# The opening of a two-layer encoder and its first w_down loads: sink values later, first weight slab first, products of zeros, four loads due earlier

## The chip, the cores and the metric

One core of a Trainium2 chip runs the whole program. The metric is the device time of one execution in microseconds (us). Five engines work side by side, each with its own queue of instructions, which it takes in order: TensorE (PE, with its weight loads as PEld), VectorE (DVE), ScalarE (ACT), GpSimd (POOL) and SyncE (SP). DMAs are issued from the queues of SP, ACT and POOL.

## What is computed

The reference is an encoder trunk of two layers over 512 tokens of width 1024, all in float32. Cut to what matters here:

```python
for l in range(DEPTH):                                   # 2
    h = rms_norm(x, attn_norm_g[l])
    qa, ka, va, qb, kb, vb, ga, gb = split(h @ w_in[l])  # 1024 x 4352
    ya = window_gqa(rope(norm(qa)), rope(norm(ka)), va, sink_a[l]) @ w_proj_a[l]
    yb = neighbourhood_attn(norm(qb), norm(kb), vb, rel_bias_b[l]) @ w_proj_b[l]
    x = x + (sigmoid(ga) * ya + sigmoid(gb) * yb) @ w_out[l]
    h = rms_norm(x, ffn_norm_g[l])
    u = silu(h @ w_gate[l]) * (h @ w_up[l])              # 1024 x 2816
    x = x + u @ w_down[l]                                # 2816 x 1024
```

## The kernel before

Activations lie transposed: the 1024 features are eight chunks of 128 partitions, the 512 tokens are the columns. Each float32 operand of a product is split in two parts, a high one rounded to the narrower type (fp32r) and a low one that holds the rest, and each product is three products on PE: high by high, high by low and low by high. The high part is made by ACT (a cast), the low part by DVE (a subtraction); for most weights the DMA itself makes it (ACT writes the negated high part, an accumulating DMA from GpSimd's queue adds the weight).

**The order of work.** The function `trunk` is run twice. In the first run nothing is emitted: an engine model with costs decides in which order the chains of attention work are placed between the main products, and which buffers of two arenas in SBUF can share a place (`Layout.pack`). In the second run the instructions are emitted in that order. Weight loads stand in a plan: `slab` gives each a due time on a running count of TensorE's work (`total`), `LEAD_H` (23 us) before use for the load and `LEAD_L` (15 us) before use for the low part, shifted by `later_h` and `later_l`. All these loads go out from GpSimd's queue, in the order in which they fall due.

**The opening.** The first product block (`token_matmul` with `begin`) starts while the input is still arriving. For each of the eight chunks k, `start(nrm, k)` turns the chunk of x that was loaded (`xin[k]`) with four transposes on PE, has ACT write the high part (`xh`, scaled by the norm's gain), the float32 copy `xT` and its square, and DVE write the low part `xl` and add up the squares; `first_parts(k)` splits the chunk's weights (ACT the cast `h`, DVE `lo`). A chunk has four groups of three products, one for each block of 128 tokens; the first group of chunk k stands before the transposes of chunk k+1 and the other three behind them. `first_load(0)` loads the first slab of w_in in two halves from ACT's queue, `first_load(1)` to `(3)` the others from GpSimd's; `x_load` loads the eight chunks of x from SP's queue. The norm gains of both norms lie in one tile `vec`, which one transpose on PE turns to columns (`vecT`). Another tile, `vec2`, holds the small gains of the heads and the token positions; it is turned by `chain_tables`, which then makes the tables of sine and cosine on DVE (it needs the constants `cst`), and which also writes `nsnk`, the negated sink values, from `snk`.

**The start of the FFN.** The blocks of w_gate and w_up are multiplied by a scheme of seven block products (`m` from `ORDER`, 24 instructions each on PE); the results of some are copied on as starting values of others (`seed`, `fetch`, `seed_c`; `seed_c` is a DVE addition that reads the bank which the next block product writes). In the first such block the low parts come by DMA from GpSimd's queue (`low_by_transfer`). Between the block products stand those with w_down (`d` steps); their four first slabs (for f0 = 0) are planned in `plan_ffn`:

```python
if c % 2 == 0:
    slab(n, 256, [(0, a["w_down"][l][P * f0 : P * (f0 + n), P * c : P * c + 256])], 0, 3.0, 2.0)
```

Of the kernel before, what the change touches and what calls it, by code (L numbers as in the profile page):

```python
# [12 lines left out]
F32 = mybir.dt.float32  # L13
# [3 lines left out]
ALU = mybir.AluOpType  # L17
AX = mybir.AxisListType

P = 128  # L20
# [4 lines left out]
NB = S // P  # L25
# [184 lines left out]
def trunk(ctx: ExitStack, tc: tile.TileContext, a: dict, out: bass.AP, lay: Layout):  # L210
    nc = tc.nc
    PS = bass.MemoryType.PSUM
    cp = ctx.enter_context(tc.tile_pool(name="cp", bufs=1))
# [7 lines left out]
    def nm(s):  # L221
        uid[0] += 1
        return f"{s}_{uid[0]}"
# [24 lines left out]
    def mm_bank():  # L248
        return pm.tile([P, S], F32, tag="mm", name=nm("mm"))

    def at_bank():
        return pa.tile([P, S], F32, tag="at", name=nm("at"))
# [83 lines left out]
    T = Engine(nc.tensor, "pe")  # L336
    V = Engine(nc.vector, "dve")
    A = Engine(nc.scalar, "act")
    G = Engine(nc.gpsimd, "pool")
    Q = Engine(nc.sync, "dma")  # L340
    AQ = Engine(nc.scalar, "dma")
# [86 lines left out]
    def at_pos(t, f):  # L428
        bisect.insort(due, (t, len(seq), f))
        seq.append(0)  # L430
# [19 lines left out]
    def slab(n, width, src, units, later_h=0.0, later_l=0.0, on_engines=False):  # L450
        i = len(plan)
        plan.append((n, width, src))
        if on_engines:
            at_pos(total[0] - LEAD_R, lambda: w_raw(i))
            at_pos(total[0] - LEAD_P, lambda: w_parts(i))
        else:
            at_pos(total[0] - LEAD_H + later_h, lambda: w_load(i))
            at_pos(total[0] - LEAD_L + later_l, lambda: w_low(i))
        total[0] += units * UNIT
# [34 lines left out]
    def plan_ffn(l):  # L494
        plan_pair(a["w_gate"][l], 0, KD, on_engines=True)
        plan_pair(a["w_up"][l], 0, KD)
        for step in ffn_steps():
            if step[0] == "m":
                _, q, w, m = step
                if m == ORDER[0]:  # L500
                    t = total[0]
                    early = 18.0 if q == 0 and w == "w_gate" else 0.0
                    quads[l, q, w] = Quad(a[w][l], 256 + 512 * q, t - early, early > 0.0)
                quads[l, q, w].due(m, total[0] - early)
                early = max(0.0, early - 1.2)
                total[0] += 24 * 0.12
            else:
                _, f0, n, c = step
                if c % 2 == 0:
                    slab(n, 256, [(0, a["w_down"][l][P * f0 : P * (f0 + n), P * c : P * c + 256])], 0, 3.0, 2.0)  # L510
                total[0] += n * UNIT

    highs, lows, raws, used = {}, {}, {}, [0]
# [1 line left out]
    def w_raw(i):  # L515

        n1, n2, ((_, ap),) = plan[i]
        raws[i] = buf([n1, n2])
        Q.dma_start(raws[i], ap.rearrange("(k p) n -> p k n", p=P))

    def w_parts(i):
        n1, n2, _ = plan[i]
        highs[i], lows[i] = buf([n1, n2], F32R), buf([n1, n2], F32R)
        A.copy(highs[i], raws[i])
        soon(lambda: V.tensor_tensor(lows[i], raws[i], highs[i].bitcast(F32), ALU.subtract), 1.2)
# [3 lines left out]
    def first_load(i):  # L529

        n1, n2, ((_, ap),) = plan[i]
        raws[i] = buf([n1, n2])
        ap = ap.rearrange("(k p) n -> p k n", p=P)
        if i:
            GQ.dma_start(raws[i], ap)
        else:
            for k in range(2):
                AQ.dma_start(raws[i][:, k], ap[:, k])
        highs[i], lows[i] = buf([n1, n2], F32R), buf([n1, n2], F32R)

    def first_parts(k):
        raw, h, lo = raws[k // 2][:, k % 2], highs[k // 2][:, k % 2], lows[k // 2][:, k % 2]
        A.copy(h, raw)
        V.tensor_tensor(lo, raw, h.bitcast(F32), ALU.subtract)

    def w_load(i):

        if i not in highs:
            n1, n2, src = plan[i]
            highs[i] = buf([n1, n2], F32R)  # L550
            for at, ap in src:
                n = ap.shape[1]
                GQ.dma_start(highs[i][:, :, at : at + n], ap.rearrange("(k p) n -> p k n", p=P))
# [133 lines left out]
    ident = cst[:, C_ID : C_ID + P]  # L687
    rev = cst[:, C_REV : C_REV + P]
    rev2 = cst[:, C_REV + 64 : C_REV + 64 + P]
    maskA = cst[:, C_MA : C_MA + 3 * P]  # L690
    vec = cp.tile([32, P], F32, tag="vec", name="vec")
    vec2 = cp.tile([P, P], F32, tag="vec2", name="vec2")
    vecT = cp.tile([P, 32], F32, tag="vecT", name="vecT")
    vec2T = cp.tile([P, P], F32, tag="vec2T", name="vec2T")
    ones = cp.tile([P, 2], F32, tag="ones", name="ones")
    magic = cp.tile([P, 32], I32, tag="magic", name="magic")
    G.memset(vec2, 0.0)
    G.memset(ones, 1.0)
    G.memset(magic, 0x5F3759DF)
# [3 lines left out]
    def x_load(c):  # L703
        t = act().rearrange("p (b n) -> p b n", b=NB)
        Q.dma_start(t, xv[:, :, P * c : P * c + P])
        xin.append(t)


    Q.dma_start(ident, a["consts"][:, :P])
    for i, n in enumerate(("attn_norm_g", "ffn_norm_g")):  # L710
        AQ.dma_start(vec[16 * i : 16 * i + 16], a[n].rearrange("l (k p) -> (l k) p", p=P))
    first_load(0)
    for c in range(KD):
        x_load(c)
    posi = cp.tile([P, P], I32, tag="posi", name="posi")
    for h in range(2):
        GQ.dma_start(
# [12 lines left out]
    gqa = cp.tile([P, 2, DEPTH, HD], F32, tag="gqa", name="gqa")  # L730
    for i, n in enumerate(("q_norm_a", "k_norm_a")):
        GQ.dma_start(gqa[:, i], a[n].rearrange("l d -> (l d)").unsqueeze(0).to_broadcast([P, DEPTH * HD]))
    snk = cp.tile([P, DEPTH, 8], F32, tag="snk", name="snk")
    GQ.dma_start(snk, a["sink_a"].rearrange("l h -> (l h)").unsqueeze(0).to_broadcast([P, DEPTH * 8]))
    GQ.dma_start(cst[:, P:], a["consts"][:, P:])
    warm = cp.tile([P, 2], F32, tag="warm", name="warm")
    A.copy(warm, ones)
    ps = at_bank()
    T.transpose(ps[:, :32], vec, ident[:32, :32])
    V.tensor_copy(vecT, ps[:, :32])  # L740

    def gain(norm, k):
        c = 16 * (norm % 2) + 8 * (norm // 2) + k
        return vecT[:, c : c + 1]

    xT = [buf([S]) for _ in range(KD)]
    nsnk = cp.tile([P, DEPTH, 8], F32, tag="nsnk", name="nsnk")
    gb = cp.tile([P, DEPTH], F32, tag="gb", name="gb")
    trig = cp.tile([P, 2, NB, 32], F32, tag="trig", name="trig")

    def chain_tables():
        yield Need("dve", [posi, snk, gqa])
        V.tensor_copy(vec2[64:68], posi[64:68])
        V.tensor_scalar(nsnk, snk, -1.0, None, ALU.mult)
        yield Need("pe", [vec2], [at_slots])
        at_slots.take()
        ps = at_bank()
        T.transpose(ps[:, :P], vec2, ident)
        yield Need("dve", [ps])
        V.tensor_copy(vec2T, ps[:, :P])  # L760
        at_slots.give(clock["dve"])
        posf = vec2T[:, 64:68]
        V.scalar_tensor_tensor(gb, vec2T[:, 0:2], HD ** -0.5, vec2T[:, 2:4], ALU.mult, ALU.mult)
        v3 = lambda t: t[:, : NB * 32].rearrange("p (b f) -> p b f", b=NB)
        ang = v3(act())
        for b in range(NB):
            V.tensor_scalar(ang[:, b, :], cst[:, C_INV : C_INV + 32], posf[:, b : b + 1], None, ALU.mult)
        yield Need()
        for i, shift in enumerate((0.25, 0.0)):
            n, r = v3(act()), v3(act())  # L770
            V.tensor_scalar(n, ang, INV_2PI, shift, ALU.mult, ALU.add)
            V.tensor_scalar(n, n, ROUND_MAGIC, None, ALU.add)
            V.tensor_scalar(n, n, -ROUND_MAGIC, None, ALU.add)
            yield Need()
            V.scalar_tensor_tensor(r, n, -TWO_PI_1, ang, ALU.mult, ALU.add)
            V.scalar_tensor_tensor(r, n, -TWO_PI_2, r, ALU.mult, ALU.add)
            V.scalar_tensor_tensor(r, n, -TWO_PI_3, r, ALU.mult, ALU.add)
            yield Need()
            if shift:
                V.tensor_scalar(r, r, HALF_PI, None, ALU.add)  # L780
            V.tensor_scalar(r, r, PI_LO, -PI_LO, ALU.min, ALU.max)
            A.activation(trig[:, i], r, AF.Sin)
            yield Need()
        done.add("trig")


# [387 lines left out]
    def start(nrm, k):  # L1174

        ps = at_bank()
        for b in range(NB):
            T.transpose(ps[:, P * b : P * b + P], xin[k][:, b, :], ident)
        if k:
            first_parts(k)  # L1180
        A.activation(held(nrm.xh[k]), by_columns(ps), AF.Copy, scale=gain(0, k))
        if not k:
            first_parts(k)
        A.copy(held(xT[k]), by_columns(ps))
        V.scalar_tensor_tensor(nrm.xl[k], xT[k], gain(0, k), nrm.xh[k].bitcast(F32), ALU.mult, ALU.subtract)
        sq = act()
        A.activation(sq, xT[k], AF.Square)
        if nrm.acc is not None:
            V.tensor_tensor(sq, sq, nrm.acc, ALU.add)
        nrm.acc = sq  # L1190
        if k == KD - 1:
            done.add("acc0")
# [528 lines left out]
```

## Time and profile before

| | before |
|---|---|
| time, median of 3 runs | 1389.4 us (1389.08 to 1389.6) |
| time of the profiled execution | 1389.13 us |
| its span, first to last instruction | 1387.4 us |
| TensorE busy in the span | 1370.7 us (99%) |
| VectorE, ScalarE, GpSimd busy | 910.7, 708.3, 317.3 us |

The profiled execution is 1.7 us longer than its span, and 0.3 us below the median. In the rows further down a time at a row's start is in us from the span's start. A row of the timeline reads: start, length, engine, line, operation, out<-in, shapes, how many were merged (x4), and in brackets how long the engine had been idle before it and what ended that. An engine with a small q (SPq, ACTq) only issues a DMA. All of the kernel's instructions are recorded at one helper's line, L310, so tiles tell them apart: `arena` is a buffer in SBUF, `at` and `mm` are banks in PSUM; where two tiles have names that differ by a number only (`vec`, `vec2`) the profile gives both as `vec`.

### The profile page before, as it was taken

The numbers are of one execution on the slowest core, as the hardware profiler recorded it, in microseconds if no ns is written. First come the engines' busy times: TensorE is split into PE (matmuls) and PEld (weight loads), VectorE is DVE, ScalarE is ACT, GpSimd is POOL, SyncE is SP. The second block draws the span as 40 slices with busy tenths as digits, with TensorE's granted clock in tenths as the row PEclk, the third lists the DMA queues.
The fourth block names the chain that finished last, engine by engine and source line by source line (L and its number), as shares of the span: only waits on it lengthen the run. The fifth ranks groups of instructions, "written<-read, shape, count | busy, mean of one in ns | idle before, by whom it ended". The sixth has DMA issues, their size and how long they took to land.

```text
span 1387.4 us, 20895 instructions
## 1 busy us (share of the span) xinstructions
PE 1370.7 (99%) x8042; PEld 1211.2 (87%) x8042; DVE 910.7 (66%) x1702; ACT 708.3 (51%) x1171; POOL 317.3 (23%) x326
## 2 busy tenths in 40 slices
PE   8999999999999999999999999999999999999998
PEld 6888888888899999999888888888888999999996
DVE  5875878555976657575648667784578757575663
ACT  6476667634643333343545675675356434333441
POOL 4542222310221110111353422223012110111110
PEclk9999999999999999999999999999999999999999
DMA  8998888864766484735899978879457583654645
GB/s 213 183 172 142 158 161 155 173 165 127 151 148 152 106 197 93 182 93 106 160 189 188 166 140 160 155 140 217 142 121 151 123 213 88 156 122 121 146 86 119
DMA packets 197331, 207.45 MB, mean 150 GB/s; under 512 B 25568, under 2 KB 167056, under 8 KB 197232
## 3 DMA queue, kind: packets, MB, share of 16 engines
q0 software_dynamic: 134976, 141.54, 54.6%
q1 hardware_dynamic: 61904, 64.04, 15.9%
q8 instruction: 63, 1.03, 0.3%
q10 hardware_dynamic: 352, 0.54, 0.1%
q14 instruction: 36, 0.29, 0.1%
HBM read 193.51 MB, written 2.10 MB: 141 GB/s over the span
## 4 chain that ended last, share of the span: by engine, by line
PE 90%; DVE 2%; issue 2%; ACT 2%; DMA 2%; POOL 0%; POOLq 0%; ACTq 0%
PE mm L310 71%; PE at L310 19%; ACT arena L310 2%; DVE arena L310 2%; DMA arena<-in_w_down 1%; DMA arena<-in_w_in 1%; DVE sm L310 0%; DMA cst<-in_consts 0%; POOL arena L310 0%; ACT L310 0%; POOL posi L310 0%; POOL vec L310 0%; DVE mm L310 0%; ACT trig L310 0%; ACT sm L310 0%
## 5 line engine op out<-in xcount | busy, mean ns | idle before, releaser
L310 PE MATMUL mm<-arena 128*128 128x512 f32 (+1 forms) x5568 | 1113.1, 355 | 5.8 <-DVE mm L310 3.4
L310 PEld LDWEIGHTS mm<-arena 128*128 128x128 f32 x5568 | 905.0, 190 | 140.7 <-DVE arena L310 4.1
L310 ACT CAST arena<-arena 128x1024 fp32r<-128x1024 f32 (+2 forms) x278 | 235.3, 869 | 213.8 <-DVE arena L310 207.7
L310 DVE TENSOR_TENSOR arena<-arena,arena 128x1024 fp32r<-128x1024 f32 (+2 forms) x268 | 262.1, 993 | 52.1 <-ACT arena L310 51.4
L310 PE MATMUL at<-arena 128*128 128x256 f32 (+1 forms) x1952 | 282.8, 289 | 0.4 <-DVE negm L310 0.4
L310 ACT ACTIVATE arena<-arena 128x1024 fp32r<-128x1024 f32 (+3 forms) x252 | 206.7, 843 | 149.4 <-DMA arena<-in_w_down 77.0
L310 PEld LDWEIGHTS at<-arena 128*128 128x128 f32 x1952 | 259.9, 191 | 13.6 <-DVE negm L310 1.4
L310 DVE TENSOR_TENSOR arena<-arena,mm 128x512 f32<-128x512 f32 x144 | 98.9, 686 | 241.8 <-PE mm L310 240.3
L310 POOL DMA_DIRECT2D arena<-in_w_in x163 | 162.2, 1370 | 303.4 <-ACT arena L310 281.7
L310 POOL DMA_DIRECT2D arena<-in_w_down x96 | 98.1, 1224 | 505.4 <-ACT arena L310 376.7
L310 DVE TENSOR_TENSOR arena<-arena 128x1024 f32<-128x1024 f32 (+4 forms) x196 | 158.0, 823 | 2.4
L310 DVE TENSOR_TENSOR arena<-at,arena 128x512 fp32r<-128x512 f32 (+4 forms) x158 | 104.3, 660 | 30.6 <-ACT arena L310 24.1
L310 ACT CAST arena<-at 128x512 fp32r<-128x512 f32 (+2 forms) x116 | 64.4, 555 | 63.7 <-PE at L310 62.4
L310 PE MATMUL at<-cst,arena 128*128 128x128 f32 x472 | 74.0, 276 | 1.8 <-issue 1.4
L310 ACT ACTIVATE arena<-arena,negm 128x256 f32<-128x256 f32 (+1 forms) x128 | 68.2, 534 | 14.4 <-DVE negm L310 12.4
L310 ACT COPY arena<-at 128x512 f32<-128x512 f32 (+1 forms) x68 | 39.5, 581 | 64.5 <-PE at L310 64.0
L310 PEld LDWEIGHTS at<-cst,arena 128*128 128x128 f32 x472 | 58.1, 141 | 11.9 <-issue 1.8
L310 DVE TENSOR_TENSOR arena<-mm,arena 128x512 f32<-128x512 f32 x72 | 49.1, 686 | 25.3 <-PE mm L310 25.1
L310 DVE CUSTOM_DVE_ANT_0 arena<-at,cst,nsnk 128x256 f32<-128x256 f32 (+1 forms) x64 | 34.4, 547 | 35.0 <-PE at L310 34.4
L310 ACT ACTIVATE arena<-arena,vecT 128x512 fp32r<-128x512 f32 x24 | 17.4, 726 | 54.8 <-DVE arena L310 54.4
L310 DVE CUSTOM_DVE_ANT_0 arena<-at,arena 128x256 f32<-128x256 f32 x64 | 26.3, 420 | 17.3 <-PE at L310 17.0
L310 POOL DMA_DIRECT2D arena<-in_w_up x8 | 8.2, 1030 | 126.7 <-PE mm L310 79.1
(68 smaller groups left out, 423.2 us busy)
## 6 DMA issues: line engine op xcount, KB each, us to landing
arena<-in_w_in POOLq DMA_DIRECT2D x99, 512.0 KB, 7.4
arena<-in_w_down POOLq DMA_DIRECT2D x80, 512.0 KB, 6.7
arena<-in_w_gate SPq DMA_DIRECT2D x20, 1024.0 KB
arena<-in_w_up SPq DMA_DIRECT2D x20, 1024.0 KB
arena<-in_w_in POOLq DMA_DIRECT2D x64, 256.0 KB, 6.4
arena<-in_w_proj_a POOLq DMA_DIRECT2D x16, 512.0 KB, 7.3
arena<-in_w_proj_b POOLq DMA_DIRECT2D x16, 512.0 KB, 7.1
arena<-in_w_out SPq DMA_DIRECT2D x16, 512.0 KB
```

The source lines that it names most:

```text
L310: f(*args, **kw)
```

## The change

Two places change. In the plan, the four first slabs of w_down in each layer fall due 10 us earlier for their load (-7.0 in place of 3.0); the due time of their low parts stays. In the opening: the first slab's two halves are the first two DMAs of ACT's queue, since the gains of the first norm go to SP's queue (second there, before x) and those of the FFN's norm to its end, behind the eight chunks of x, and into 16 partitions of `vec2`, so `vecT` has 16 columns and `gain` reads the FFN's gains from `vec2T`. `nsnk` is written at the end of `chain_tables`. The weights of chunk 0 are split before x's high part is written. And PE multiplies a tile of zeros by itself: seven times at the start, three times behind the transposes of chunk 0 (`trig` serves as the zero tile until its values are written).

```diff
-                    slab(n, 256, [(0, a["w_down"][l][P * f0 : P * (f0 + n), P * c : P * c + 256])], 0, 3.0, 2.0)
+                    slab(n, 256, [(0, a["w_down"][l][P * f0 : P * (f0 + n), P * c : P * c + 256])], 0, 3.0 if f0 else -7.0, 2.0)
...
+    trig = cp.tile([P, 2, NB, 32], F32, tag="trig", name="trig")
+    idle = trig[:, 0].rearrange("p b f -> p (b f)")
+
+    def turn_over(n):
+
+        ps = mm_bank()
+        for _ in range(n):
+            T.matmul(ps[:, :P], idle, idle, start=True, stop=True)
+
+    G.memset(idle, 0.0)
     G.memset(vec2, 0.0)
...
+    first_load(0)
     Q.dma_start(ident, a["consts"][:, :P])
-    for i, n in enumerate(("attn_norm_g", "ffn_norm_g")):
-        AQ.dma_start(vec[16 * i : 16 * i + 16], a[n].rearrange("l (k p) -> (l k) p", p=P))
-    first_load(0)
+    Q.dma_start(vec, a["attn_norm_g"].rearrange("l (k p) -> (l k) p", p=P))
     for c in range(KD):
         x_load(c)
+    Q.dma_start(vec2[32:48], a["ffn_norm_g"].rearrange("l (k p) -> (l k) p", p=P))
...
+    turn_over(7)
     ps = at_bank()
-    T.transpose(ps[:, :32], vec, ident[:32, :32])
-    V.tensor_copy(vecT, ps[:, :32])
+    T.transpose(ps[:, :16], vec, ident[:16, :16])
+    V.tensor_copy(vecT, ps[:, :16])
...
     def gain(norm, k):
-        c = 16 * (norm % 2) + 8 * (norm // 2) + k
-        return vecT[:, c : c + 1]
+        t, c = (vec2T, 32) if norm % 2 else (vecT, 0)
+        c += 8 * (norm // 2) + k
+        return t[:, c : c + 1]
...
     def chain_tables():
-        yield Need("dve", [posi, snk, gqa])
+        yield Need("dve", [posi])
         V.tensor_copy(vec2[64:68], posi[64:68])
-        V.tensor_scalar(nsnk, snk, -1.0, None, ALU.mult)
         yield Need("pe", [vec2], [at_slots])
...
+        yield Need("dve", [snk, gqa])
+        V.tensor_scalar(nsnk, snk, -1.0, None, ALU.mult)
         done.add("trig")
...
         for b in range(NB):
             T.transpose(ps[:, P * b : P * b + P], xin[k][:, b, :], ident)
-        if k:
-            first_parts(k)
+        if not k:
+            turn_over(3)
+        first_parts(k)
         A.activation(held(nrm.xh[k]), by_columns(ps), AF.Copy, scale=gain(0, k))
-        if not k:
-            first_parts(k)
         A.copy(held(xT[k]), by_columns(ps))
```

How the instructions stand on three queues follows. A row names the operation, what it writes and reads, the shape of the output, and in brackets the semaphores that it waits for: those named DMA.. tell that a transfer has landed, those named for an engine that one of its instructions is done.

TensorE in the opening, before. `at<-cst,vec` is the transpose of the norm gains, `at<-cst,arena` the four transposes of a chunk of x, `mm<-arena` the products, and `at_181<-cst,vec_76` the transpose of `vec2`:

```order
L310 MATMUL at_140<-cst,arena_72 128x128 x3
L310 MATMUL mm_122<-arena_73 128x512 x3
L310 MATMUL mm_123<-arena_73 128x512 x3
L310 MATMUL mm_124<-arena_73 128x512 x3
L310 MATMUL mm_121<-arena_73 128x512 [waits Activation_49]
L310 MATMUL mm_121<-arena_73 128x512 [waits DVE_49] x2
L310 MATMUL at_166<-cst,arena_72 128x128 [waits DMAHW7_49]
L310 MATMUL at_166<-cst,arena_72 128x128 x3
L310 MATMUL mm_122<-arena_73 128x512 x3
L310 MATMUL at_181<-cst,vec_76 128x128 [waits DMASW5_49,DMASW3_49,DMASW6_49,DMASW2_49,DVE_49]
L310 MATMUL mm_123<-arena_73 128x512 x3
```

The same place now, from the transposes of chunk 2 (`at_178`) on:

```order
L310 MATMUL mm_130<-arena_73 128x512 [waits Activation_49]
L310 MATMUL mm_130<-arena_73 128x512 [waits DVE_49] x2
L310 MATMUL at_178<-cst,arena_72 128x128 [waits DMAHW6_49]
L310 MATMUL at_178<-cst,arena_72 128x128 x3
L310 MATMUL at_190<-cst,vec_76 128x128 [waits DMASW5_49,DMASW6_49,DMASW3_49,DMAHW4_49,DMASW2_49,DVE_49]
L310 MATMUL mm_131<-arena_73 128x512 x3
L310 MATMUL mm_132<-arena_73 128x512 x3
L310 MATMUL mm_133<-arena_73 128x512 x3
L310 MATMUL mm_130<-arena_73 128x512 [waits Activation_49]
L310 MATMUL mm_130<-arena_73 128x512 [waits DVE_49] x2
L310 MATMUL at_211<-cst,arena_72 128x128 [waits DMAHW7_49]
```

The transpose of `vec2` stands three products earlier, directly behind the transposes of chunk 2, and it has one more wait, DMAHW4. That is the second use of that semaphore, the transfer of the FFN's gains into `vec2`. Nine products of chunk 1 and the first three of chunk 2 stand between it and the transposes of chunk 3 (`at_211`).

SP's queue at the start, now; before, it had the constants and the eight chunks of x alone:

```order
L310 DMA cst<-in_consts 128x128
L310 DMA vec<-in_attn_norm_g 16x128
L310 DMA arena_72<-in_x 128x4x128 x4
L310 DMA arena_72<-in_x 128x4x128 [waits DMAHW0_49]
L310 DMA arena_72<-in_x 128x4x128 [waits DMAHW1_49]
L310 DMA arena_72<-in_x 128x4x128 [waits DMAHW2_49]
L310 DMA arena_72<-in_x 128x4x128 [waits DMAHW3_49]
L310 DMA vec_76<-in_ffn_norm_g 16x128 [waits DMAHW4_49,Pool_49]
```

The gains of the FFN's norm, which ACT's queue issued second, are now the tenth transfer of SP's.

GpSimd's queue at the start of the FFN, before. `arena<-arena` are the transfers that make low parts (`low_by_transfer`), `in_w_down 128x2x256` the loads of the first slabs and of their low parts:

```order
L310 DMA arena_73<-arena_72 128x1024 [waits DMAHW1_49,DMAHW2_49,DMAHW0_49,DMAHW3_49,DMASW5_49,DMAHW6_49,DVE_49,Activation_49]
L310 DMA arena_73<-arena_72 128x4x256 [waits DMAHW1_49,DMAHW3_49,DMASW6_49,DMAHW6_49,DVE_49,Activation_49]
L310 DMA arena_73<-arena_72 128x4x256 [waits DMASW7_49,Activation_49]
L310 DMA arena_73<-arena_72 128x4x256 [waits DMAHW1_49,DMASW0_49,DMAHW4_49,DVE_49,Activation_49]
L310 DMA arena_73<-in_w_down 128x2x256 [waits DMAHW6_49,DMASW1_49]
L310 DMA arena_73<-arena_72 128x4x256 [waits DMASW2_49,PE_49,Activation_49]
L310 DMA arena_73<-in_w_down 128x2x256 [waits DMASW3_49,PE_49,Activation_49]
L310 DMA arena_73<-in_w_down 128x2x256 [waits DMASW4_49,PE_49]
```

And now:

```order
L310 DMA arena_73<-arena_72 128x1024 [waits DMAHW1_49,DMAHW2_49,DMAHW0_49,DMAHW3_49,DMASW5_49,DMAHW6_49,DVE_49,Activation_49]
L310 DMA arena_73<-in_w_down 128x2x256 [waits DMASW6_49]
L310 DMA arena_73<-arena_72 128x4x256 [waits DMAHW1_49,DMASW7_49,DMAHW3_49,DVE_49,DMAHW6_49,PE_49,Activation_49]
L310 DMA arena_73<-arena_72 128x4x256 [waits DMASW0_49,PE_49,Activation_49]
L310 DMA arena_73<-in_w_down 128x2x256 [waits DMASW1_49]
L310 DMA arena_73<-arena_72 128x4x256 [waits DMAHW1_49,DMASW2_49,DMAHW4_49,DVE_49,Activation_49]
L310 DMA arena_73<-arena_72 128x4x256 [waits DMASW3_49,PE_49,Activation_49]
L310 DMA arena_73<-in_w_down 128x2x256 [waits DMASW4_49,PE_49]
```

The load of slab 0 stands three transfers earlier, and that of slab 1 (the last row before) ahead of two transfers more; both wait only for older transfers of the same queue. The same holds in layer 1. On ACT, VectorE and TensorE the order at this place is as before.

## Rows read from the trace of the kernel before

**Rows 1.** The page, its first part: busy time of each engine, share of the span and number of instructions.

```profile
PE 1370.7 (99%) x8042; PEld 1211.2 (87%) x8042; DVE 910.7 (66%) x1702; ACT 708.3 (51%) x1171; POOL 317.3 (23%) x326
```

**Rows 2.** The waits of TensorE over the whole span: who waited for whom, us in total, times, the longest.

```profile
PE at L310 <- DMA vec<-in_ffn_norm_g: 4.1, 1, 4.1
PE mm L310 <- DVE mm L310: 3.4, 2, 1.7
```

**Rows 3.** The timeline around the start of the FFN in layer 0, engine by engine (POOL, then ACT, VectorE and TensorE), and last the piece of the chain of work that holds the transfer.

```profile
356.83 0.86 POOL L310 DMA_DIRECT2D arena<-arena  x1 [0.85 <-DVE sm L310]
...
372.44 1.27 POOL L310 DMA_DIRECT2D arena<-arena  x1 [1.67 <-DVE arena L310]
...
379.91 0.63 ACT L310 ACTIVATE arena<-arena 128x512 fp32r<-128x512 f32 x1 [1.81 <-DMA arena<-in_w_down]
...
377.95 2.42 DVE L310 TENSOR_TENSOR arena<-arena 128x1024 f32<-128x1024 f32 x3
381.99 2.36 DVE L310 TENSOR_TENSOR arena<-arena,arena 128x1024 fp32r<-128x1024 f32 x2 [1.63 <-ACT arena L310]
...
385.40 0.69 DVE L310 TENSOR_TENSOR mm<-mm,arena 128x512 f32<-128x512 f32 x1
...
381.55 3.04 PE L310 MATMUL at<-arena 128*128 128x256 f32 x24
386.24 10.01 PE L310 MATMUL mm<-arena 128*128 128x256 f32 x76 [1.66 <-DVE mm L310]
...
373.19 6.70 DMA arena<-in_w_down
```

**Rows 4.** The same place in layer 1, from the timelines of VectorE and TensorE.

```profile
1066.04 0.69 DVE L310 TENSOR_TENSOR mm<-mm,arena 128x512 f32<-128x512 f32 x1
...
1062.12 3.04 PE L310 MATMUL at<-arena 128*128 128x256 f32 x24
```

**Rows 5.** The timeline of the opening, all engines: DMA issues, and what ACT and VectorE do for the first chunks.

```profile
1.20 6.67 SPq L310 DMA_DIRECT2D arena<-in_x  x8
...
1.66 1.09 ACTq L310 DMA_DIRECT2D arena<-in_w_in  x2
...
6.14 0.61 ACT L310 CAST arena<-arena 128x512 fp32r<-128x512 f32 x1
...
12.04 0.54 POOL L310 DMA_DIRECT2D cst<-in_consts  x1 [1.90 <-DMA arena<-in_w_in]
12.45 0.22 DVE L310 CAST vec<-posi 4x128 f32<-4x128 int32 x1
...
16.72 0.17 DVE L310 TENSOR_SCALAR nsnk<-snk 128x16 f32<-128x16 f32 x1 [4.05 <-DMA snk<-in_sink_a]
...
19.07 0.67 DVE L310 TENSOR_SCALAR arena<-cst,vec2T 128x32 f32<-128x32 f32 x4
...
20.38 0.75 DVE L310 SCALAR_TENSOR_TENSOR arena<-arena,vecT,arena 128x512 fp32r<-128x512 f32 x1
```

**Rows 6.** The timeline of the opening, TensorE: transposes (`at`) and products (`mm`).

```profile
4.40 1.12 PE L310 MATMUL at<-cst,arena 128*128 128x128 f32 x4
6.80 2.18 PE L310 MATMUL mm<-arena 128*128 128x512 f32 x3 [1.28 <-ACT arena L310]
...
9.48 4.53 PE L310 MATMUL mm<-arena 128*128 128x512 f32 x12
13.86 0.60 PE L310 MATMUL at<-cst,arena 128*128 128x128 f32 x4
...
17.55 0.50 PE L310 MATMUL mm<-arena 128*128 128x512 f32 x1 [0.68 <-DVE arena L310]
...
18.55 0.60 PE L310 MATMUL at<-cst,arena 128*128 128x128 f32 x4
18.90 3.02 PE L310 MATMUL mm<-arena 128*128 128x512 f32 x12
```

**Rows 7.** The instructions that read the tile `ones`, TensorE's among them: float32 products of one column, 16 in the program (four in each of four norms); how many records, and ns (least, median, most).

```profile
L310 PE MATMUL at<-ones,arena x32: 164/250/250, 36.2 to 1035.0; 128*128 128x1 f32 x32
```

**Rows 8.** DMA queues by stretch (q0 is GpSimd's, q1 SP's): packets, MB moved, share of 16 engines' time. In order: q1 in 0 to 9 us; q0 and q1 in 9 to 14; q1 in 14 to 17; q1 in 17 to 18; and, of the first 30 us, the issue of the constants with its size and its us to landing.

```profile
q1 hardware_dynamic: 2915, 1.45, 58.2%
...
q0 software_dynamic: 477, 1.53, 85.2%
q1 hardware_dynamic: 581, 0.29, 20.7%
...
q1 hardware_dynamic: 833, 0.41, 52.0%
...
q1 hardware_dynamic: 39, 0.02, 6.5%
...
cst<-in_consts POOLq DMA_DIRECT2D x1, 336.0 KB, 6.7
```

**Rows 9.** Busy time by stretch: in the opening from 2 to 3 us, in the FFN's start from 380 to 390, and near the end of the span. Columns: stretch, its us, busy us (and instructions) of PE, PEld, DVE, ACT, POOL, granted TensorE clock as a share of full speed, busy share of the DMA engines, GB/s.

```profile
2.00:3.00 1.00, 0.00 (x0) 0.00 (x0) 0.00 (x0) 0.22 (x1) 1.00 (x3) 1.00 0.48 135
...
380.00:390.00 10.00, 8.35 (x70) 8.17 (x69) 7.41 (x9) 6.12 (x9) 2.34 (x3) 1.00 0.80 177
...
1383.00:1384.00 1.00, 0.09 (x1) 0.00 (x0) 0.00 (x0) 0.59 (x1) 0.00 (x0) 1.00 0.61 185
...
1385.00:1386.00 1.00, 0.00 (x0) 0.00 (x0) 0.00 (x0) 0.00 (x0) 0.00 (x0) 0.50 0.53 169
```

More of the change, by code (lines that the diff above doesn't have):

```diff
@@ L690, in trunk @@
     maskA = cst[:, C_MA : C_MA + 3 * P]
-    vec = cp.tile([32, P], F32, tag="vec", name="vec")
+    vec = cp.tile([16, P], F32, tag="vec", name="vec")
     vec2 = cp.tile([P, P], F32, tag="vec2", name="vec2")
-    vecT = cp.tile([P, 32], F32, tag="vecT", name="vecT")
+    vecT = cp.tile([P, 16], F32, tag="vecT", name="vecT")
     vec2T = cp.tile([P, P], F32, tag="vec2T", name="vec2T")
@@ L748, in trunk @@
     gb = cp.tile([P, DEPTH], F32, tag="gb", name="gb")
-    trig = cp.tile([P, 2, NB, 32], F32, tag="trig", name="trig")
     def chain_tables():
-        yield Need("dve", [posi, snk, gqa])
+        yield Need("dve", [posi])
         V.tensor_copy(vec2[64:68], posi[64:68])
-        V.tensor_scalar(nsnk, snk, -1.0, None, ALU.mult)
         yield Need("pe", [vec2], [at_slots])
```

## The prediction, made before the changed kernel ran

> **What bounds the kernel now.** The page first: TensorE is busy for 1370.7 of 1387.4 us [rows 1], so only work that PE does slower than it could, or time in which PE waits, can be won or lost. Then PE's waits over the span: the reader is to see that the first load of the gains costs 4.1 us and that VectorE (DVE) is waited for twice, 3.4 us together [rows 2]; these two are the FFN's starts. Last the two stretches by time.
>
> At the FFN's start in layer 0, PE ends a block product at 381.55 + 3.04 = 384.59 and goes on only at 386.24. It waits for `seed_c`, which DVE ends at 385.40 + 0.69 = 386.09. DVE is late because it idled 1.63 us before 381.99, for ACT; ACT idled 1.81 us until 379.91, for slab 0 of w_down, whose negated high part it writes. That transfer runs from 373.19 for 6.70 us, to 379.89, on the dot [rows 3]. Layer 1 repeats it: 1062.12 + 3.04 = 1065.16 against 1066.04 + 0.69 = 1066.73 [rows 4].
>
> In the opening three things hold PE: the wait for the first transfers (4.06 us), a wait of 1.28 for ACT, and gaps of 0.68 and 0.16 for DVE at 17.55 and 18.21; beside them the lower clock. Twelve products take 4.53 us at 9.48 and 3.02 us at 18.90; four transposes take 1.12 at 4.40 and 0.60 at 13.86 [rows 6]. These are PE's levels of 1.2 and 2.4 GHz, as far as durations tell them; the clock column reads 1.00 already in 2 to 3 us, before PE's first instruction [rows 9], and is no guide there.
>
> **The w_down loads.** GpSimd issued slab 0's load behind the transfer of 372.44. Now it stands right behind the one of 356.83, which ends issuing at 357.69. With the same 6.70 us it lands near 364.4; ACT asks for it 1.81 before 379.91, at 378.10: over 13 us to spare. Slab 1 goes out ahead of the transfer of 372.44, in front of which GpSimd idled 1.67 us, so it delays nothing, and lands some 7 us later, near 378, while ACT turns to it only behind slab 0's work. So the 1.81 goes. What is late next is DVE's own work: it ends three subtractions at 377.95 + 2.42 = 380.37, so its idle time shrinks from 1.63 to about nothing. `seed_c` then ends 1.62 sooner, at 384.47, before PE's 384.59. PE gets back its whole 1.66, or all but 0.1 of it. In layer 1 `seed_c` ends at 1065.1 against PE's 1065.16: 1066.73 − 1065.16 and the step after it, 1.6 to 1.7. The two waits together are 3.4 [rows 2]; I take **−3.2**, bounds −3.4 and −2.9 (some 0.25 per layer that stays because the extra transfers lie beside others in a stretch with a DMA share of 0.80 [rows 9]). The moved loads wait only for older transfers of their queue, so no new wait stands in front of the low parts.
>
> **The opening, before the wait that is new.** (a) x's first chunk goes out one SP issue later (6.67 / 8 = 0.83 at most, about 0.4 for a small one); against it the cast of 0.61, which ACT made at 6.14 behind x's high part and for which PE's first product waited, now lies ahead of it and beside the transposes [rows 5]. They cancel within 0.5. (b) The zeros: a float32 product leaves two records (16 of them leave 32 [rows 7]), each like a transpose of 128 columns at the lower clock, at 0.28 us (1.12 / 4), or 0.15 at the higher one (0.60 / 4). Seven take 2.1 to 3.9 us from about 1 us on, so they end at 3.1 to 4.9, beside a start wait of 4.06; three take 0.9 to 1.7 beside PE's 1.28 for ACT [rows 6]. What is not hidden, up to 0.8 and 0.4, goes into the slack of the next part. (c) The higher level comes sooner, since PE works from 1 us on and not from 4.4: the products of chunk 1 cost 3.0 in place of 4.5. (d) `nsnk`, for whose operand DVE idled 4.05 us until 16.72 [rows 5], leaves the way; the gaps of 0.68 and 0.16 go with it.
>
> All of (a) to (d) only moves the moment at which PE comes to the transpose of `vec2`: before that was about 15 (13.86 + 0.60 and three products of 0.25), now it is about 12.7: 1.5 less by (c), and 0.75 less for three products that stand behind the transpose instead of ahead of it. I keep 11.5 to 14.5, for chunk 0's products (2.18 for three) can gain from the level too, and (a) and (b) can cost.
>
> **The wait that is new.** That transpose now needs the FFN's gains, the last of SP's ten transfers, behind all of x. PE works in order; behind it are queued nine products of chunk 1, three of chunk 2 and the transposes of chunk 3, for which ACT and then DVE wait. When does the last of SP's queue land? SP's queue moved 1.45 MB by 9 us, 0.29 in 9 to 14 (beside 1.53 of GpSimd's), 0.41 in 14 to 17 and its last 0.02 between 17 and 18 [rows 8]. So x alone was complete at about 17.2. What pulls this in is the first slab of w_in, whose two halves were issued from 1.66 at 0.55 each [rows 5], behind two issues of gains: without them some 0.9 sooner, in a stretch where the DMA engines were busy to 0.48 [rows 9]: some 0.1 MB sooner in all, and at 0.41 / 3 = 0.14 MB a us that is 0.7 us. The gains land at about 16.5. Bounds: 15.5 (the early bytes are worth twice that) and 18.3 (nothing gained, and a full issue more).
>
> The Trainium skill, "DMA: Bandwidth & Descriptors", section "Queues, rings and completion order", says that each DMA engine takes turns between the queue rows packet by packet and takes a row's descriptors in ring order; the trace agrees as far as it goes, with 581 packets of SP's queue beside 477 of GpSimd's in 9 to 14 us [rows 8]. By that rule the small transfer cannot pass x; could it, the third rival below would hold.
>
> Behind the wait, twelve products of 3.02 us stand ahead of chunk 3's transposes: 16.5 + 0.1 + 3.0 = 19.6 at the higher level, against 18.55 before [rows 6]. From there PE had work without a gap, so this goes through to the end: **+1.05**, bounds 0 and +2.8.
>
> **The clock in that wait.** PE idles 2 to 5 us. At the end of the span its last instruction stands in 1383 to 1384 (0.09 us busy), and the clock is 0.50 in 1385 to 1386; in 380 to 390, with an idle stretch of 1.66, it stayed at 1.00 [rows 9]. A wait of 2 to 5 us is nearer the former, so I take it that the clock falls, and that the twelve products behind cost 4.53 and not 3.02: **+1.5**, bounds 0 and +2.2 (half as much again, if the lower level lasts on into chunk 3).
>
> The Trainium skill, "TensorE: Matmul & The Clock Gate", section "HAM oscillation — how this bites in real kernels", describes a product loop in which a wait for DMA between bursts lets the clock go back to half. By that the sum is −0.65, without it about −2.2; the end of this trace, 0.50, goes with it.
>
> **What the opening could win at best.** Without the wait for the gains DVE is next: it needs the constants, issued at 12.04 with 6.7 to landing, 18.7 [rows 5, 8]; then 0.67, 0.68 and 0.75 stand ahead of chunk 3's low part, 20.8 at the earliest, against 20.38 + 0.75 = 21.13. So at most about 0.4 is won, or 1.2 if the constants too come 0.8 sooner.
>
> **The sum.** −3.2 + 1.05 + 1.5 = −0.65 against the profiled execution of 1389.13: 1388.5. The median of the runs is 0.3 above it, so I forecast **1388.7** against 1389.4. About 0.2%, 2.8 us, is what a measurement of this kernel can tell from no change.
>
> **The rivals.**
> - *Likeliest (0.40):* as summed; 1387.8 to 1389.6 by itself.
> - *The clock stays up (0.20):* PE waits for the gains, but at 1.00, as in 380 to 390. −3.2 + 1.05 = −2.15: 1387.2, 1386.3 to 1388.2. Against it is the length of the wait; for it, that PE's seven and three zeros move the fall as well as the rise.
> - *The gains come in time (0.20):* they land by 15.6, so that 15.6 + 3.0 = 18.6 is no later than before, or the clock makes it up. The opening gives 0 to −1.2 and the sum is −3.2 to −4.4: 1386.2 to 1385.0, taken as 1385.8. It speaks for it that SP's queue moved only 0.43 MB behind 14 us; against it, that GpSimd's queue is as full as before.
> - *Slower (0.11):* the gains land as late as 18.3, and the clock is down. 18.3 + 4.5 = 22.8 in place of 18.55 is +4.3, less 3.2 is +1.1; with the lower level on into chunk 3, +1.8: 1390.5 to 1391.2. It decides from a landing of 17.2 with the clock down (17.2 + 4.5 − 18.55 = 3.15, as much as the FFN gives).
> - *The w_down edit does not do what it says (0.09):* PE's 1.66 stays, since another wait of DVE or ACT ends as late (the low parts by transfer, say, now beside more traffic). The opening's +2.5 stands alone: 1391.9.
>
> **Range and chances.** 1385.5 to 1391.0 holds some 0.82 of this. Faster by over 0.2% means below 1386.6: the third case nearly whole and a little of the second, 0.24. Slower means above 1392.2: half of the last case's spread and the far end of the slower one, 0.06. The rest, 0.70, is within.
>
> **What would show it.** In the changed trace: ACT's two waits of 1.81 for w_down and DVE's 1.63 gone, and PE's 1.66 with them; if slab 0 has landed but PE still waits, the next late thing was missed. A PE wait that ends with the transfer of the FFN's gains into `vec2`: its length tells (c), its end the landing (16.5), and twelve products behind it in 3.0 or 4.5 tell the clock. Chunk 3's transposes at 19.6 (clock up) or 21.1 (down) against 18.55 give the opening's term at once. `nsnk` without its 4.05. The prediction is wrong if the wait for the gains is under 1 us, if PE's time at chunk 7 is not moved by what chunk 3 shows, or if a new wait stands at the FFN's start.

## The result and the profile after

The changed kernel takes 1392.58 us in the median against 1389.38 of the kernel before in the same comparisons: a ratio of 1.0022 with a 95% interval of 1.0013 to 1.0030, 3.2 us slower. The forecast was 1388.7, with a range to 1391.0.

The profiled execution takes 1391.64, the fastest of the 13 runs and 0.9 under the median. TensorE (PE) is busy for 4.4 us more than in [rows 1], in the first part of the page; the ten products of zeros are the 20 records more:

```profile
PE 1375.1 (99%) x8062; PEld 1216.2 (88%) x8062; DVE 910.6 (66%) x1702; ACT 707.3 (51%) x1171; POOL 318.0 (23%) x327
```

The waits of PE answer [rows 2] (who waited for whom, us in total, times, the longest). The two waits of 1.7 for VectorE (DVE) are gone, and at the head stands one transfer, once. The row has the name of the first one of [rows 2], but there it was the wait for the first transfers, until 4.09; here it is the transpose of `vec2` at 18.91. The 1.5 for DVE stands at the end of the span, where the kernel before has 1.42:

```profile
PE at L310 <- DMA vec<-in_ffn_norm_g: 5.4, 1, 5.4
PE at L310 <- DVE arena L310: 1.8, 2, 1.5
```

**The FFN's start**, to be read beside [rows 3]: the timeline of ACT, VectorE and PE in layer 0.

```profile
383.68 0.64 ACT L310 ACTIVATE arena<-arena 128x512 fp32r<-128x512 f32 x1
...
386.05 2.36 DVE L310 TENSOR_TENSOR arena<-arena,arena 128x1024 fp32r<-128x1024 f32 x2
...
389.46 0.69 DVE L310 TENSOR_TENSOR mm<-mm,arena 128x512 f32<-128x512 f32 x1
...
387.16 3.04 PE L310 MATMUL at<-arena 128*128 128x256 f32 x24
390.30 4.90 PE L310 MATMUL mm<-arena 128*128 128x256 f32 x39
```

ACT writes slab 0's negated high part without a wait, DVE goes on without one, `seed_c` ends at 390.15 and PE, which is done at 390.20, goes on at 390.30. All of it stands later by what the opening lost, but PE's stretch is 1.55 us shorter: 387.16 is 5.61 behind its row of before, 390.30 only 4.06 behind its own. Layer 1 repeats it (the two rows follow one another): PE ends the block at 1066.13 + 3.04 = 1069.17 and goes on at 1069.27, 0.10 later, where it waited 1.72 before.

```profile
1066.13 3.04 PE L310 MATMUL at<-arena 128*128 128x256 f32 x24
1069.27 5.99 PE L310 MATMUL mm<-arena 128*128 128x256 f32 x48
```

**The opening**, to be read beside [rows 6]: PE's timeline.

```profile
1.00 3.35 PE L310 MATMUL mm<-trig 128*128 128x128 f32 x14 [1.00 <-POOL trig L310]
...
5.51 1.12 PE L310 MATMUL at<-cst,arena 128*128 128x128 f32 x4 [0.94 <-DMA arena<-in_x]
...
9.96 3.07 PE L310 MATMUL mm<-arena 128*128 128x512 f32 x12
...
12.87 0.60 PE L310 MATMUL at<-cst,arena 128*128 128x128 f32 x4
...
18.91 0.45 PE L310 MATMUL at<-cst,vec 128*128 128x128 f32 x1 [5.43 <-DMA vec<-in_ffn_norm_g]
...
19.01 5.20 PE L310 MATMUL mm<-arena 128*128 128x512 f32 x12
...
24.05 0.60 PE L310 MATMUL at<-cst,arena 128*128 128x128 f32 x4
24.40 3.00 PE L310 MATMUL mm<-arena 128*128 128x512 f32 x12
```

PE is through the transposes of chunk 2 at 13.47 and stands until 18.91 for the FFN's gains. The twelve products behind take 5.20 us, those behind chunk 3's transposes 3.00. Chunk 3's transposes, the last row but one, come at 24.05 and not at 18.55: 5.5 us late, and chunk 7's, at 37.74 against 32.25, are late by the same. The granted clock in the same stretch (columns as in [rows 9]):

```profile
13.00:14.00 1.00, 0.47 (x5) 0.23 (x3) 0.84 (x2) 0.49 (x1) 0.10 (x1) 1.00 1.05 367
...
16.00:17.00 1.00, 0.00 (x0) 0.00 (x0) 0.06 (x1) 0.00 (x0) 0.00 (x0) 0.96 1.17 366
17.00:18.00 1.00, 0.00 (x0) 0.00 (x0) 0.00 (x0) 0.00 (x0) 0.00 (x0) 0.50 1.65 351
...
23.00:24.00 1.00, 1.00 (x4) 0.80 (x3) 0.00 (x0) 0.00 (x0) 0.00 (x0) 0.63 0.00 0
24.00:25.00 1.00, 1.00 (x8) 0.86 (x7) 0.00 (x0) 0.32 (x1) 0.00 (x0) 1.00 0.00 0
```

It falls to 0.50 (1.2 GHz) while PE idles, stays there for nearly all of the twelve products, and is back at 1.00 (2.4 GHz) in 24 to 25.

### The profile page after: what moved, and what is told of

Read it like the earlier page. It is cut to its first block, busy times and chain, and to the rows that moved or that the text cites. A ratio compares the mean times of both kernels' runs of the same rounds, so it can differ in the third digit from the quotient of the medians.

```text
span 1389.9 us, 20947 instructions
## 1 busy us (share of the span) xinstructions
PE 1375.1 (99%) x8062; PEld 1216.2 (88%) x8062; DVE 910.6 (66%) x1702; ACT 707.3 (51%) x1171; POOL 318.0 (23%) x327
## 4 chain that ended last, share of the span: by engine, by line
PE 92%; ACT 2%; DMA 2%; issue 2%; DVE 1%; POOL 1%; SPq 0%; DVEq 0%; POOLq 0%; ACTq 0%
PE mm L310 72%; PE at L310 20%; ACT arena L310 2%; DMA arena<-in_w_in 1%; DVE arena L310 1%; DMA vec<-in_ffn_norm_g 1%; POOL arena L310 1%; SPq L310 0%; ACT L310 0%; ACT trig L310 0%; DVEq L1728 0%; ACT sm L310 0%; DVE sm L310 0%; DVE den L310 0%; POOLq L310 0%
## 5 line engine op out<-in xcount | busy, mean ns | idle before, releaser
L310 DVE CUSTOM_DVE_ANT_0 arena<-at,arena 128x256 f32<-128x256 f32 x64 | 26.3, 420 | 17.2 <-PE at L310 16.9
L310 ACT ACTIVATE arena<-arena,vec2T 128x512 fp32r<-128x512 f32 x16 | 11.6, 726 | 47.5 <-DVE arena L310 47.5
```

The source lines that it names most:

```text
L310: f(*args, **kw)
```

## Experiments

Times are medians; before is 1389.3 to 1389.5 beside them. The theory (G): the FFN edit gives what was forecast, and the whole loss is the place of one load, the FFN's gains at the end of SP's queue: a wait, and the clock that falls in it.

**The two halves apart.** The FFN edit alone is the first hunk of the diff put into the kernel before; the opening alone is the changed kernel with 3.0 put back.

> The kernel before with the w_down edit alone. Theory G (the FFN edit works as forecast, the whole loss is in the opening): TensorE's two waits of 1.66 and 1.72 for VectorE go, the opening is that of before, time 3.2 to 3.4 us under before, 1386.1. Rival F (the earlier loads take from other transfers what they give, and the changed kernel's loss has a part there): 1388 to 1390, with a new wait in the FFN's stretch.

> The changed kernel with the old due time of the w_down slabs, so the opening's part alone. Theory G: the opening costs what it cost in the changed kernel, chunk 3's transposes at about 24 us and not at 18.55, +5.5 to +6.5: 1395 to 1396. Rival F: less, +3 to +4, 1393, since part of the loss would lie in the FFN's stretch.

Measured: 1385.97 (ratio 0.9972, 0.9962 to 0.9982) and 1396.10 (1.0048, 1.0035 to 1.0061): −3.5 and +6.6, together +3.1, the change's +3.2. So the halves don't touch each other, and rival F falls.

**The gains sooner.** Of the changed kernel, one load is moved:

```diff
     first_load(0)
+    AQ.dma_start(vec2[32:48], a["ffn_norm_g"].rearrange("l (k p) -> (l k) p", p=P))
...
         x_load(c)
-    Q.dma_start(vec2[32:48], a["ffn_norm_g"].rearrange("l (k p) -> (l k) p", p=P))
```

> The changed kernel, but the FFN's gains go out third on ACT's queue, behind the first slab's two halves, and not last on SP's; all else stays. Theory G (the 5.4 us wait for these gains and the clock that falls in it are the whole loss): no wait at the transpose of vec2, clock 1.00 throughout; VectorE then waits for the constants until about 18.05 and ends chunk 3's low part near 20.2 (21.1 before), so the opening gives 0 to 0.9 and the time is 1385.2 to 1386.1. Rival Z (the zeros, the later x and the new order of chunk 0 cost time by themselves, and the wait only covers it): 1388 to 1391.

Measured: 1385.39 (0.9969, 0.9956 to 0.9981), 7.2 us under the changed kernel. PE's timeline of this kernel shows the transpose of `vec2` without a wait, and chunk 3's transposes at 16.35, 2.2 us sooner than before the change:

```profile
13.48 0.27 PE L310 MATMUL at<-cst,vec 128*128 128x128 f32 x1
...
13.51 3.00 PE L310 MATMUL mm<-arena 128*128 128x512 f32 x12
...
16.35 0.60 PE L310 MATMUL at<-cst,arena 128*128 128x128 f32 x4
...
32.00 0.60 PE L310 MATMUL at<-cst,arena 128*128 128x128 f32 x4
```

The last row is chunk 7's; in the kernel before it reads so:

```profile
32.25 0.60 PE L310 MATMUL at<-cst,arena 128*128 128x128 f32 x4
```

So of 2.2 us at chunk 3 only 0.25 is left at chunk 7. In this kernel DVE's timeline shows the first that takes it back, the constants:

```profile
18.26 0.68 DVE L310 TENSOR_SCALAR arena<-cst,vec2T 128x32 f32<-128x32 f32 x4 [1.63 <-DMA cst<-in_consts]
```

**That one load alone.** The kernel before, with only the gains' load moved to the end of SP's queue and into `vec2` (the `gain` and `vecT` lines of the diff go with it):

> The kernel before, with one thing of the change alone: the FFN's gains go to the end of SP's queue and into vec2. No zeros, w_in's halves and the order of chunk 0 as before, sink values and w_down as before. Theory G (the place of this one load is enough for the loss): TensorE comes to the transpose of vec2 at about 15 us, waits until 17.5 to 18.9, the clock falls, nine products behind it at the lower level: chunk 3's transposes at 21.5 to 23, time 1392 to 1394. Rival S (the first slab, sooner, is what pushed x and the gains back): the gains land by 17, +1 at most, 1390.4.

Measured: 1395.46 (1.0034, 1.0021 to 1.0048), +6.0, nearly the whole +6.6 of the opening, and above the 1392 to 1394 that were expected. PE's timeline:

```profile
5.89 1.12 PE L310 MATMUL at<-cst,arena 128*128 128x128 f32 x4 [2.82 <-DMA arena<-in_x]
...
20.10 0.30 PE L310 MATMUL at<-cst,vec 128*128 128x128 f32 x1 [3.40 <-DMA vec<-in_ffn_norm_g]
```

The gains land here at about 20, in this execution later than in the changed kernel's, although w_in's halves are only one issue sooner than before; chunk 0 of x comes at 5.89 and not at 4.40, since that one issue already puts the halves ahead of x (SP's queue moved 0.06 MB in 3 to 4 us). The later x is not the loss: in the kernel without the zeros, further down, it comes at 5.88 and nothing is lost, so rival S falls. Taking the load away from its place removes the loss, and putting it there alone makes it.

**Its place in the queue.** In the changed kernel the load is put ahead of the last chunk of x (the diff), and behind the fourth (with 4 for the 7):

```diff
     for c in range(KD):
+        if c == 7:
+            Q.dma_start(vec2[32:48], a["ffn_norm_g"].rearrange("l (k p) -> (l k) p", p=P))
         x_load(c)
-    Q.dma_start(vec2[32:48], a["ffn_norm_g"].rearrange("l (k p) -> (l k) p", p=P))
```

> The changed kernel with one DMA swapped: on SP's queue the FFN's gains go out ahead of the last chunk of x and not behind it. Theory T (the gains land late because they are the tail of SP's queue, whose last packets trickle in beside GpSimd's loads): SP's queue moved 0.39 MB in 14 to 17 us, so 0.26 MB less ahead of the gains is 2 us or more: landing 15.5 to 17, a wait of 2 to 3.5 us, the clock falls or not, chunk 3's transposes at 19 to 21, time 1387 to 1389. Rival Q (a small transfer on this queue is late at any place): 1392 to 1393.

> As e9_gains_before_x7, with the gains behind the fourth chunk of x, four chunks sooner. Theory T: they land by about 12 us, before TensorE asks at 13.5: no wait, the time of e3_gains_early, 1385.4 within 0.5. Rival Q: 1391 to 1393.

Measured: 1389.96 (1.0005, 0.9996 to 1.0014) and 1385.05 (0.9970, 0.9959 to 0.9981). The second is as expected and has the lowest median of all, 4.2 us under before and 7.5 under the changed kernel; the first lies a little above its 1387 to 1389. PE's rows of the first, where the gains land at 17.4:

```profile
17.39 0.44 PE L310 MATMUL at<-cst,vec 128*128 128x128 f32 x1 [4.63 <-DMA vec<-in_ffn_norm_g]
17.48 5.22 PE L310 MATMUL mm<-arena 128*128 128x512 f32 x12
```

and of the second, at the same two instructions:

```profile
13.22 0.27 PE L310 MATMUL at<-cst,vec 128*128 128x128 f32 x1
13.25 3.04 PE L310 MATMUL mm<-arena 128*128 128x512 f32 x12
```

In the profiled executions one chunk of x sooner gave 1.5 us of landing (18.9 to 17.4), against the 2 us or more that were expected (the medians differ by 2.6), and the price follows the place: rival Q falls.

**The clock's part.** Twenty products of zeros are put into the wait (the diff), then 32. They don't change when the gains land.

```diff
         ps = at_bank()
+        for _ in range(20):
+            T.matmul(ps[:, :P], idle, idle, start=True, stop=True)
         T.transpose(ps[:, :P], vec2, ident)
```

> The changed kernel with 20 more products of zeros directly ahead of the transpose of vec2, some 5 us of work in the 5.4 us wait; the wait's end, the landing of the gains near 18.8 us, is not touched. Theory G (of the opening's loss, 2.0 to 2.2 are the clock and 3.5 the wait): clock 1.00 in 17 to 24 us, the twelve products behind in 3.0 and not 5.2 us, time 1390.4. Rival K (those products are slow for another reason, or the loss is all wait, DVE being late anyway): 1392.6 as the changed kernel. Rival Z2 (the extra products themselves run past the landing): 1393 or more.

> As e4_wait_filled, with 32 products of zeros and not 20: they end near 20.5 us, behind the landing of the gains, so that no idle time is left whenever the gains land. Theory G (the clock that falls in the wait is about 2 us of the loss): clock 1.00 from 14 to 25 us, the twelve products in 3.0, chunk 3's transposes at 23.5 although the products start 1.5 us later than in the changed kernel; time 1391.0, under the changed kernel's 1392.6. Rival K (the products behind are slow whatever stands ahead of them): 20.5 + 5.2, 1393 or more.

Measured: 1390.53 (1.0008, 0.9999 to 1.0017) and 1391.13 (1.0010, 1.0001 to 1.0019), both at the numbers of theory G. For the first the profiled execution, of 1391.67, doesn't bear the reason out: the zeros end at 17.7, the gains land only at 19.6, and the clock, still 1.00 in what is left of the wait, falls just behind it, with PE at work again: the last two rows (columns as in [rows 9]) read 1.00 in 18 to 19 and 0.50 in 20 to 21.

```profile
13.09 4.63 PE L310 MATMUL at<-trig 128*128 128x128 f32 x40
19.63 0.30 PE L310 MATMUL at<-cst,vec 128*128 128x128 f32 x1 [1.91 <-DMA vec<-in_ffn_norm_g]
19.68 4.59 PE L310 MATMUL mm<-arena 128*128 128x512 f32 x12
...
18.00:19.00 1.00, 0.00 (x0) 0.00 (x0) 0.00 (x0) 0.00 (x0) 0.00 (x0) 1.00 1.76 359
...
20.00:21.00 1.00, 1.00 (x3) 0.73 (x3) 0.97 (x7) 0.00 (x0) 0.00 (x0) 0.50 0.23 44
```

Where the gain of this kernel's median comes from, this trace, 1.1 us above the median, doesn't show. The second settles that the clock has a price; its PE has no idle time until behind the landing, the clock is 1.00 in each microsecond from 14 to 25, and the twelve products take 3.03:

```profile
14.14 7.31 PE L310 MATMUL at<-trig 128*128 128x128 f32 x64
...
21.31 3.03 PE L310 MATMUL mm<-arena 128*128 128x512 f32 x12
```

Here the products start 2.3 us later than in the changed kernel and chunk 3's transposes come at 24.18 against 24.05: 2.2 us are the clock's in the changed kernel's profiled execution. The median is 1.45 under the changed kernel's.

**What bounds the opening without the wait.** Three kernels: the gains early and the constants' load ahead of the slabs of chunks 4 to 7; the gains early without the zeros; and the FFN edit with the late sink values as the opening's only edit.

> The kernel of e3_gains_early, and beside it the constants' load (336 KB, GpSimd's queue) goes out ahead of the slabs of chunks 4 to 7 and not behind them. Theory D (with the gains early, VectorE's wait of 1.63 us for the constants until 18.26 is what takes back the 2.2 us that chunk 3's transposes came sooner): the wait goes, the opening keeps 0.5 to 1.5 us more, 1384.0 to 1384.9. Rival B (VectorE's own work in the opening, or x, which the constants now delay, bounds it): no gain against 1385.4, or slower.

> The kernel of e3_gains_early without the ten products of zeros. Theory D: the higher clock level comes only near 13 us, TensorE is up to 1.5 us later at the transpose of vec2, but VectorE waits for the constants until 18.2 in any case: within 0.4 of 1385.4. Rival Z (the zeros are worth their clock): 1386.5 to 1387.

> The kernel of e1_ffn_only, and of the opening's edits one alone: the sink values are negated at the end of the tables' chain. Theory D (the constants and not the sink values bound VectorE): VectorE's 4 us until 16.7 go, TensorE's gaps behind them and with them the clock that fell in e1's profiled execution; 0.2 to 0.8 under e1's 1386.0, 1385.2 to 1385.8, as much as the whole opening gives with the gains early. Rival N (they were no burden): 1386.0. Rival O (it takes the zeros and the first slab too): over 1385.8, above the 1385.4 of e3_gains_early.

Measured: 1385.23 (0.9966, 0.9953 to 0.9978), 1385.40 (0.9967, 0.9954 to 0.9979) and 1385.78 (0.9972, 0.9962 to 0.9983). All three, and e3's 1385.39, lie within their intervals of each other. With the constants early, DVE's wait for them is gone, and the next thing stands on ACT, a slab of w_in that its in-order queue waits for; behind it PE waits 0.47 us for ACT:

```profile
16.67 0.67 DVE L310 TENSOR_SCALAR arena<-cst,vec2T 128x32 f32<-128x32 f32 x4
...
20.69 1.06 ACT L310 ACTIVATE arena<-arena 128x1024 fp32r<-128x1024 f32 x1 [1.69 <-DMA arena<-in_w_in]
```

Without the zeros PE comes to the transpose of `vec2` at 14.97 and not at 13.48, and nothing is lost at the end. With the sink values late and nothing else, DVE's 4.05 of [rows 5] is replaced by a wait for the constants:

```profile
19.34 0.68 DVE L310 TENSOR_SCALAR arena<-cst,vec2T 128x32 f32<-128x32 f32 x4 [2.32 <-DMA cst<-in_consts]
```

What the late sink values are worth by themselves is open: 1385.78 against the 1385.97 of the FFN edit alone is within what these runs can tell.

## Why the prediction was wrong

**The w_down loads: right.** −3.2 was forecast, −3.5 measured alone; in the profiled executions the two starts give 1.55 and 1.62. The waits of ACT, DVE and PE went as described, and `seed_c` ends just ahead of PE.

**The new wait: right in place, wrong in size.** The prediction named the transpose of `vec2`, what is queued behind it and chunk 3's transposes as the measure. PE came there at 13.5, inside the 11.5 to 14.5. The step that failed is the landing: "at about 16.5", with bounds of 15.5 and 18.3; it was 18.9 in the profiled execution, 19.4, 19.6 and 20.1 in those of e2, e4 and e8. (The bounds' own terms make 15.8 and 18.0: 17.2 less twice 0.7, and 17.2 with an issue of 0.83.) Three readings were at fault.

The first is the 0.7 us: w_in's halves, sooner, were to fill idle DMA engines and so pull x in. They took the engines that x had. In 3 to 4 us SP's queue (q1) before the change had the engines nearly alone (packets, MB, share of 16 engines' time):

```profile
q1 hardware_dynamic: 584, 0.29, 97.0%
```

and after it, ACT's (q10) beside it:

```profile
q10 hardware_dynamic: 176, 0.31, 82.4%
q1 hardware_dynamic: 137, 0.06, 21.7%
```

x's first chunk came at 5.51 in place of 4.40. In these two traces that was made up later, though: by 14 us SP's queue had moved 1.77 MB against 1.74 before, and at 17 it had 46 packets left against 39. So the 0.7 was not gained, but the 1.7 us from 17.2 to 18.9 were not lost here either. (By 9 us it had moved 1.37 MB and not 1.45; but e1, whose opening is that of before, had moved 1.36.)

The second is the end of the queue. 17.2 was read from [rows 8] at a rate of 0.14 MB a us up to the last byte, and in that one execution it is nearly right: SP's packets of 17 to 18 us went in 17 to 17.2 and in 17.2 to 17.4.

```profile
q1 hardware_dynamic: 27, 0.01, 22.7%
...
q1 hardware_dynamic: 12, 0.00, 9.9%
```

It does not hold from one execution to the next. The same queue, in the two other traces of the opening as it was, still moved packets behind 19: e1 has 88, 16 and 1 in 17 to 18, 18 to 19 and 19 to 20, e11 47, 7 and 5. There it cost nothing, since chunk 7 of x is not wanted before 32 us. The queues after the change in 17 to 18 us and in 18 to 19:

```profile
q0 software_dynamic: 330, 0.33, 156.4%
q1 hardware_dynamic: 42, 0.02, 8.9%
...
q0 software_dynamic: 358, 0.36, 180.8%
q1 hardware_dynamic: 4, 0.00, 0.8%
```

Beside GpSimd's 330 packets the last few dozen of SP's take more than a microsecond, until 18.2. The change put a load that PE wants at 13.5 behind this trickle. The Trainium skill ("DMA: Bandwidth & Descriptors", section "Queues, rings and completion order") lets each engine take turns between queues packet by packet; by that, 42 packets beside 330 would mean that on most engines SP's queue was done and a few were behind. That is argued, not shown: why the last packets are so slow was not tried, and the traces don't tell the engines apart.

The third stood at nothing: the time of the last packets was taken for the landing. The last ones went in 18 to 18.2, and by the chain of work the transfer landed only at 7.50 + 11.27 = 18.77:

```profile
7.50 11.27 DMA vec<-in_ffn_norm_g
```

Together: 0.7 not gained, some 0.9 of trickle (17.2 to 18.1) and some 0.8 from there to PE's start at 18.91 make the 2.4 us between 16.5 and 18.9.

**The clock: right that it falls, short in price.** +1.5 was forecast from 4.53 against 3.02; the products took 5.20, which with their overlap into the next transposes is 2.05 to 2.2, the upper bound. For them the lower level held nearly to the end. The 4.53 was not a price of the lower level alone: in the trace of before these products start at 11.34, 11.77 and 12.19, 0.43 us apart, but at 12.92 and 13.16, 0.24 apart, so the level rose among them; twelve at 0.43 make the 5.2. The price also differs: 5.22 in e9, 4.72 in e2, 4.59 in e4.

**The sum.** By the profiled executions the opening cost 3.45 by the wait (18.91, 0.1 and 3.0 make 22.0 against 18.55) and 2.05 by the clock (24.05 against 22.0), 5.5 where +2.55 stood; less 3.2 in the FFN's two starts that is 2.3 of the span's 2.5 (1389.9 against 1387.4). So of the miss 2.4 us are the wait's term and 0.55 the clock's. The medians differ by 3.2, 0.7 more than the spans; no trace shows where that lies. A later landing alone doesn't make it: in e2's trace the gains land at 19.39, and chunk 3's transposes still come at 24.05. The mechanism is that of the "slower" rival, which had 0.11 and ended at 1391.2 because its landing stopped at 18.3.

**What the opening could win: nearly right.** 0.4 at best was forecast, by the constants; with the gains early chunk 7 comes 0.25 sooner than before in the profiled execution of e3, 0.40 and 0.70 sooner in those of e5 and e6, 0.11 later in e10's; the medians of e3, e5 and e6 are 0.6 to 0.7 under the FFN edit alone, e10's 0.9, differences within the intervals. The zeros win their clock (twelve products in 3.07 at 9.96) but not time. In (a), x's first chunk was 1.1 later and not 0.4.

## What to carry to other kernels

A load is not small because its bytes are few: before it is moved behind a long queue, read when that queue's last packet goes, in more than one execution, when the transfer counts as landed, and who waits in order behind the load. Where the DMA engines are already full, a transfer that starts sooner takes its bytes from another; say which. And count what an idle TensorE costs twice, in the wait and in the products behind it, for which the price stands in rows of the same products at either clock; see first that such a row is not a mixture of both.

## What the runs showed of the hardware

Idle time far shorter than the change's can be followed by the lower clock. In the profiled execution of the FFN edit alone, whose opening is that of before, PE idled 1.34 us for DVE, and the clock then read 0.50 from 19 to 22 us:

```profile
18.06 0.50 PE L310 MATMUL mm<-arena 128*128 128x512 f32 x1 [1.34 <-DVE arena L310]
```

```profile
18.00:19.00 1.00, 0.78 (x2) 0.47 (x3) 1.00 (x3) 0.00 (x0) 0.00 (x0) 0.94 1.65 358
19.00:20.00 1.00, 1.00 (x6) 0.84 (x5) 0.97 (x6) 0.00 (x0) 0.00 (x0) 0.50 1.56 292
```

The execution took 1387.74, 1.8 over its median. In the FFN's start a wait of 1.66 left the clock at 1.00 [rows 3, 9]. So the length of one wait, as read here, doesn't decide alone; the kernel before carries this risk in its opening too. Of its 15 runs beside e5 to e8 four have a mean granted clock of 0.998 and take 1391.2 to 1391.6 us, the others 0.999 or 1.000 and at most 1390.8; that the clock fell at this place in the four is not shown.

Nor need the clock fall in the wait that goes before. In the rows above PE has gone on at 18.06, and the clock reads 0.94 in 18 to 19. With the gains late alone (e8) PE idles 3.40 us until 20.10 at 1.00, goes on at 1.00, and the clock falls only in 21 to 22:

```profile
20.00:21.00 1.00, 0.90 (x5) 0.78 (x6) 0.53 (x4) 0.00 (x0) 0.00 (x0) 1.00 0.67 128
21.00:22.00 1.00, 1.00 (x5) 0.76 (x4) 1.00 (x5) 0.00 (x0) 0.00 (x0) 0.63 0.17 31
```

Its nine products take 3.29 us; twelve take 3.0 at the higher level. So what a wait costs in clock is read from the products behind it, and not from the clock within it.
